# Hardware loops on three engines, and a ring of 96 rows, in an RMSNorm and swish kernel

## The chip, the cores and the metric

The kernel runs on one core of one Trainium2 chip. The metric is the device time of one execution in microseconds (us), of which lower is better. A core has engines that run their own instruction streams and meet at semaphores: TensorE (PE), VectorE (DVE), ScalarE (ACT), GpSimd (POOL) and SyncE (SP), which here only issues transfers. Sixteen DMA engines move data between HBM and the on-chip memories; in this trace every transfer of SP lands in sixteen parts, one for each of them, and the parts land in the order of issue.

## The reference

The input `x` has 16 x 1024 rows of 512 float32 numbers. Each row is normalized by its root mean square, multiplied by `gamma`, and passed through swish:

```python
rms = np.sqrt(np.mean(x ** 2, axis=-1, keepdims=True) + eps)
x_norm = x / rms * gamma
return (x_norm * (1.0 / (1.0 + np.exp(-x_norm)))).astype(np.float32)
```

So 33.55 MB are read and 33.55 MB are written, with little arithmetic on each number.

## The kernel before

**Tiling.** The 16384 rows are laid over 128 partitions, so each partition has 128 rows ("rows" below are these: one row is 128 x 2 KB = 256 KB of data). They come in eight groups of 16 rows per partition, and within a group the 16 rows of a partition lie together in HBM: a transfer of 16 rows has pieces of 32 KB, one of 4 rows has pieces of 8 KB, each 32 KB from the next. `xb` is a ring in SBUF with room for `ring = 100` rows; a row is loaded, worked on in place and stored from its place.

**Transfers.** `loads` and `stores` are lists of (first row, number of rows), and `order` is the order in which SP issues them, all on one queue. `load` (the transfer is issued at L121) makes SP wait for the store that frees the ring's places, and `store` (L127) waits for the swish of the store's last rows. With 100 places, the nine loads of rows 0 to 99 are issued at once, then the three stores of rows 0 to 31, then the three loads of rows 100 to 127, each behind one of these stores, then the other eight stores.

**Units.** `cn = 4` rows are a unit, so there are K = 32 units. For each unit:

- ACT, `square(k)`: waits for the landing, squares two rows with their sums accumulated (L170, output to `junk`, two instructions a row in the profile), and squares the other two rows at once into `sq` in PSUM (L177);
- DVE, `sums(k)`: adds up `sq` (L205) and so completes `ms`;
- POOL: adds `eps` (L151) and raises to the power -0.5 (L158), which gives `rstd`;
- DVE, `norm(k)`: four instructions, one a row, `x * rstd * gamma` (L216);
- ACT, `swish(k)`: Silu over the four rows (L189), in place.

ACT runs `square(k)` and then `swish(k - 2)`; DVE runs `sums(k)` and then `norm(k - 1)`. All of it is written out unit by unit: no engine has a loop at run time, and each wait is for a count that grows with the unit. `ms`, `aeps` and `rstd` have a place for every unit, `sq` and `junk` have two buffers each, and the writers of `sq` and `junk` wait for their former readers (`s_sum`, `s_acc`).

Of the kernel before, what the change touches and what calls it, by code (L numbers as in the profile page):

```python
# [9 lines left out]
def kernel(  # L10
# [7 lines left out]
    nc = tc.nc  # L18
    P = nc.NUM_PARTITIONS
    AF = mybir.ActivationFunctionType  # L20
    ALU = mybir.AluOpType
    fp32 = mybir.dt.float32
# [3 lines left out]
    R, D = xf.shape  # L26

    groups = [16] * 8
    ring = 100
    loads = [(0, 4), (4, 4), (8, 8), (16, 16), (32, 16), (48, 16), (64, 16), (80, 16)]  # L30
    loads += [(96, 4), (100, 12), (112, 12), (124, 4)]
    stores = [(0, 16), (16, 8), (24, 8), (32, 16), (48, 16), (64, 16), (80, 16)]
    stores += [(96, 4), (100, 12), (112, 8), (120, 8)]
    order = [("load", i) for i in range(loads.index((100, 12)))]
    order += [("store", t) for t in range(3)]
    order += [("load", i) for i in range(loads.index((100, 12)), len(loads))]
    order += [("store", t) for t in range(3, len(stores))]
    early = 2
    cn = 4
    n_sq = 2  # L40

    first = [sum(groups[:g]) for g in range(len(groups))]
    rows_each = sum(groups)
# [6 lines left out]
        assert sum(n for _, n in pieces) == rows_each  # L50

    K = rows_each // cn
    landings, seen = [], 0
    for k in range(K):
        landings.append([])
# [6 lines left out]
    inv_d = 1.0 / float(D)  # L62
    eps_f = float(eps)
# [4 lines left out]
    def sbuf(name, shape, dt=fp32):  # L68
        return nc.alloc_sbuf_tensor(name, shape, dt).ap()

    xb = sbuf("xb", [P, ring, D])
    gamma4 = sbuf("gamma4", [P, D])
    gamma_sb = sbuf("gamma_sb", [P, D])
    neg_half = sbuf("neg_half", [P, cn])
    ms = sbuf("ms", [P, K, cn])
    aeps = sbuf("aeps", [P, K, cn])
    rstd = sbuf("rstd", [P, K, cn])
    sq = [nc.alloc_psum_tensor(f"sq{i}", [P, n_sq, D], fp32).ap() for i in range(2)]
    junk = [nc.alloc_psum_tensor(f"junk{i}", [P, D], fp32).ap() for i in range(2)]

    ld = [nc.alloc_semaphore(f"ld{t}") for t in range(len(loads))]
    st = [nc.alloc_semaphore(f"st{t}") for t in range(len(stores))]
    s_gld = nc.alloc_semaphore("s_gld")
    s_zero = nc.alloc_semaphore("s_zero")
    s_half = nc.alloc_semaphore("s_half")
    s_gamma = nc.alloc_semaphore("s_gamma")
    s_acc = nc.alloc_semaphore("s_acc")
    s_sq = nc.alloc_semaphore("s_sq")
    s_sum = nc.alloc_semaphore("s_sum")
    s_eps = nc.alloc_semaphore("s_eps")  # L90
    s_rstd = nc.alloc_semaphore("s_rstd")
    s_norm = nc.alloc_semaphore("s_norm")
    s_swish = nc.alloc_semaphore("s_swish")

    def need(ins, sem, value):
        return ins.wait_op(sem, value, "sem-ge")
# [17 lines left out]
    def load(i):  # L114
        a, n = loads[i]
        for u, (c, m) in enumerate(stores):
            over = c + ring < a + n and a < c + m + ring
            if over and u not in stored_by_sync:
                nc.sync.wait_ge(st[u], 16)
                stored_by_sync.add(u)  # L120
        return nc.sync.dma_start(  # L121
            out=buf(loads[i]), in_=dram(xf, loads[i])
        ).then_inc(ld[i], 16)

    def store(t):
        need(
            nc.sync.dma_start(out=dram(of, stores[t]), in_=buf(stores[t])),  # L127
            s_swish, ends[t],
        ).then_inc(st[t], 16)
# [3 lines left out]
    for t in range(early):  # L133
        ins = load(t).ins
        assert here[-1] is ins or here[-1].name == ins.name
        here.pop()
        at = next(
            i for i, other in enumerate(entry)
            if other.engine == mybir.EngineType.SP
            and isinstance(other, mybir.InstDrain)  # L140
        )
        entry.insert(at, ins)
    for what, t in order[early:]:
        load(t) if what == "load" else store(t)

    nc.gpsimd.memset(gamma4, 0.0).then_inc(s_zero, 1)  # L146
    nc.gpsimd.memset(neg_half, -0.5).then_inc(s_half, 1)  # L147
    nc.gpsimd.wait_ge(s_half, 1)
    for k in range(K):
        need(  # L150
            nc.gpsimd.tensor_scalar(  # L151
                out=aeps[:, k, :], in0=ms[:, k, :], scalar1=eps_f, scalar2=None,
                op0=ALU.add,
            ),
            s_sum, k + 1,
        ).then_inc(s_eps, 1)
        need(
            nc.gpsimd.tensor_tensor(  # L158
                out=rstd[:, k, :], in0=aeps[:, k, :], in1=neg_half, op=ALU.pow
            ),  # L160
            s_eps, k + 1,
        ).then_inc(s_rstd, 1)

    def square(k):
        at = k * cn % ring
        for landing in landings[k]:
            nc.scalar.wait_ge(ld[landing], 16)  # L167
        for j in range(n_sq, cn):
            n = k * (cn - n_sq) + j - n_sq
            acc = nc.scalar.activation(  # L170
                out=junk[n % 2], in_=xb[:, at + j, :], func=AF.Square,
                scale=inv_d**0.5, accum_out=ms[:, k, j : j + 1],
            )
            if n >= 2:
                need(acc, s_acc, n - 1)
            acc.then_inc(s_acc, 1)
        square = nc.scalar.activation(  # L177
            out=sq[k % 2], in_=xb[:, at : at + n_sq, :],
            func=AF.Square, scale=inv_d**0.5,
        )  # L180
        if k >= 2:
            need(square, s_sum, k - 1)
        square.then_inc(s_sq, 1)

    def swish(k):
        at = k * cn % ring
        rows = xb[:, at : at + cn, :]
        need(
            nc.scalar.activation(out=rows, in_=rows, func=AF.Silu), s_norm, k + 1  # L189
        ).then_inc(s_swish, 1)  # L190

    need(
# [1 line left out]
        s_zero, 1,  # L194
    ).then_inc(s_gld, 16)
    nc.scalar.preload_act_table_set("silu_and_others")  # L196
    for k in range(K + 2):
        if k < K:
            square(k)
        if k >= 2:  # L200
            swish(k - 2)

    def sums(k):
        need(
            nc.vector.tensor_reduce(  # L205
                out=ms[:, k, 0:n_sq], in_=sq[k % 2], op=ALU.add,
                axis=mybir.AxisListType.X,
            ),
            s_sq, k + 1,
        ).then_inc(s_sum, 1)  # L210

    def norm(k):
        at = k * cn % ring
        for j in range(cn):
            row = xb[:, at + j, :]
            ins = nc.vector.scalar_tensor_tensor(  # L216
                out=row, in0=row, scalar=rstd[:, k, j : j + 1], in1=gamma_sb,
                op0=ALU.mult, op1=ALU.mult,
            )
            if j == 0:  # L220
                need(ins, s_rstd, k + 1)
        ins.then_inc(s_norm, 1)

    for k in range(K + 1):
        if k < K:
            sums(k)
        if k == 0:
            need(
                nc.vector.stream_shuffle(gamma_sb, gamma4, [0] * 32), s_gld, 16  # L229
            ).then_inc(s_gamma, 1)  # L230
        if k == 1:
            nc.vector.wait_ge(s_gamma, 1)
        if k >= 1:
            norm(k - 1)

    for t in range(len(stores)):
        if t not in stored_by_sync:
# [36 lines left out]
```

## Time and profile before

| what | us |
|---|---|
| median of three runs (lowest, highest) | 161.36 (161.28, 161.55) |
| the profiled execution | 161.94 |
| its span, first to last instruction | 160.6 |
| its last swish ends | 140.42 |
| its last store is issued | 140.4 |

The span is what the profile's views show; 1.3 us of the profiled execution lie outside of it. "DMA share" in a table of windows is the busy time of the transfers' packets over sixteen engines' time; a packet counts where it ends, so a single microsecond may show more than 1. A row such as `q1 hardware_dynamic: 3312, 67.11, 98.1%` gives packets, MB and share of one queue; q1 is SP's. The trace also records when each of a transfer's sixteen parts has landed. For some of the transfers (us from the span's start; first and last part):

| transfer | issued | first part landed | last part landed |
|---|---|---|---|
| load (0, 4) | 0.00 | 4.25 | 4.78 |
| load (32, 16) | 2.76 | 31.14 | 31.55 |
| load (48, 16) | 3.24 | 40.86 | 41.71 |
| load (64, 16) | 3.86 | 50.58 | 51.62 |
| load (80, 16) | 4.38 | 60.28 | 61.34 |
| load (96, 4) | 4.86 | 63.30 | 65.17 |
| store (0, 16) | 30.04 | 72.99 | 74.88 |
| load (112, 12) | 79.75 | 97.31 | 99.20 |
| load (124, 4) | 84.62 | 99.80 | 102.42 |
| store (80, 16) | 109.88 | 138.44 | 141.14 |
| store (112, 8) | 133.82 | 153.03 | 155.73 |
| store (120, 8) | 140.45 | 157.90 | 160.58 |

### The profile page before, as it was taken

To read this page: it belongs to the slowest core of one execution; us is meant where nothing else is said; L and a number is where in the kernel's file an instruction comes from. 1 tells how busy PE (TensorE), PEld (TensorE's weight loads), DVE (VectorE), ACT (ScalarE), POOL (GpSimd) and SP (SyncE) were. 2 spreads that over 40 slices of the span, in tenths; PEclk is the share of its full clock that TensorE was granted. 3 is DMA by queue.
4 is the path that set the end of the run, shared out by engine and by line. 5 is a ranking of instruction groups with operands and counts; after the bars stand their busy time and mean duration, and the time that the engine had idled before them with its cause. 6 is when DMAs were issued, how large, how long until landed. Compare 5 with 4: busy or idle time off the path is not lost.

```text
span 160.6 us, 503 instructions
## 1 busy us (share of the span) xinstructions
DVE 124.5 (78%) x162; ACT 129.6 (81%) x193; POOL 65.4 (41%) x70
## 2 busy tenths in 40 slices
DVE  0287959999999999999999999999999999400000
ACT  1939959999999999999999999999999994700000
POOL 1053545555555555555555555555555555000000
DMA  7999999999999999999999999999999999899993
GB/s 263 449 465 392 498 416 392 481 432 392 453 449 400 424 404 369 459 424 392 426 453 447 410 435 433 435 465 408 424 475 408 400 490 416 369 451 437 428 420 139
DMA packets 3324, 67.15 MB, mean 418 GB/s; under 512 B 372, under 2 KB 372, under 8 KB 376
## 3 DMA queue, kind: packets, MB, share of 16 engines
q1 hardware_dynamic: 3312, 67.11, 98.1%
q14 instruction: 4, 0.03, 0.0%
q10 hardware_dynamic: 8, 0.01, 0.0%
HBM read 33.56 MB, written 33.55 MB: 418 GB/s over the span
## 4 chain that ended last, share of the span: by engine, by line
ACT 63%; DMA 12%; issue 7%; DVE 4%; SPq 0%; ACTq 0%
ACT xb L189 25%; ACT junk L170 22%; ACT sq L177 16%; DMA xb<-in_x_dram 12%; DVE xb L216 3%; DVE ms L205 1%; SPq L121 0%; ACTq L167 0%
## 5 line engine op out<-in xcount | busy, mean ns | idle before, releaser
L216 DVE SCALAR_TENSOR_TENSOR xb<-xb,rstd,gamma_sb 128x512 f32<-128x512 f32 x128 | 87.3, 745 | 0.0
L189 ACT ACTIVATE xb<-xb 128x2048 f32<-128x2048 f32 x32 | 60.9, 1903 | 2.8 <-DVE xb L216 2.8
L205 DVE TENSOR_REDUCE ms<-sq 128x2 f32<-128x1024 f32 x32 | 39.2, 1225 | 14.0 <-ACT sq L177 10.6
L151 POOL TENSOR_SCALAR aeps<-ms 128x4 f32<-128x4 f32 x32 | 20.6, 645 | 65.6 <-DVE ms L205 65.6
L158 POOL TENSOR_TENSOR rstd<-aeps,neg_half 128x4 f32<-128x4 f32 x32 | 44.0, 1376 | 2.7
L170 ACT ACTIVATE junk<-xb 128x512 f32<-128x512 f32 x64 | 37.2, 582 | 4.5 <-DMA xb<-in_x_dram 4.5
L177 ACT ACTIVATE sq<-xb 128x1024 f32<-128x1024 f32 x32 | 32.2, 1005 | 0.0
L170 ACT ACTIVATION_READ_ACCUMULATOR junk<-xb 128x1 f32 x64 | 11.9, 186 | 0.0
L196 ACT ACT_TABLE_LOAD x1 | 1.3, 1283 | 3.6 <-issue 3.6
L146 POOL MEMSET gamma<- 128x512 f32 x1 | 0.5, 525 | 1.5 <-POOLq L66 1.5
L229 DVE STREAM_SHUFFLE gamma_sb<-gamma 128x512 f32<-128x512 f32 x1 | 0.7, 720 | 0.0
L255 POOL MEMSET const-float32-0.0<- 128x1 f32 x1 | 0.1, 99 | 0.2 <-issue 0.2
L255 POOL MEMSET const-bfloat16-1.0<- 128x1 bf16 x1 | 0.1, 102 | 0.0
L255 POOL MEMSET const-uint8-127<- 128x1 uint8 x1 | 0.1, 102 | 0.0
L147 POOL MEMSET neg_half<- 128x4 f32 x1 | 0.1, 102 | 0.0
L255 POOL MEMSET const-float32-1.0<- 128x1 f32 x1 | 0.1, 98 | 0.0
L229 DVE LOAD_MASK_SELECT gamma_sb<-gamma x1 | 0.0, 15 | 0.0
## 6 DMA issues: line engine op xcount, KB each, us to landing
xb<-in_x_dram SPq DMA_DIRECT2D x5, 4096.0 KB, 38.5
out_dram<-xb SPq DMA_DIRECT2D x5, 4096.0 KB, 36.3
out_dram<-xb SPq DMA_DIRECT2D x4, 2048.0 KB, 30.2
xb<-in_x_dram SPq DMA_DIRECT2D x2, 3072.0 KB, 18.2
xb<-in_x_dram SPq DMA_DIRECT2D x4, 1024.0 KB, 12.3
out_dram<-xb SPq DMA_DIRECT2D x1, 3072.0 KB, 25.0
xb<-in_x_dram SPq DMA_DIRECT2D x1, 2048.0 KB, 10.2
out_dram<-xb SPq DMA_DIRECT2D x1, 1024.0 KB, 29.7
```

The lines of the kernel that those rows point to most:

```text
L146: nc.gpsimd.memset(gamma4, 0.0).then_inc(s_zero, 1)
L147: nc.gpsimd.memset(neg_half, -0.5).then_inc(s_half, 1)
L151: nc.gpsimd.tensor_scalar(out=aeps[:, k, :], in0=ms[:, k, :], scalar1=eps_f, scalar2=None, op0=ALU.add,),
L158: nc.gpsimd.tensor_tensor(out=rstd[:, k, :], in0=aeps[:, k, :], in1=neg_half, op=ALU.pow),
L170: acc = nc.scalar.activation(out=junk[n % 2], in_=xb[:, at + j, :], func=AF.Square, scale=inv_d**0.5, accum_out=ms[:, k, j : j + 1],)
L177: square = nc.scalar.activation(out=sq[k % 2], in_=xb[:, at : at + n_sq, :], func=AF.Square, scale=inv_d**0.5,)
L189: nc.scalar.activation(out=rows, in_=rows, func=AF.Silu), s_norm, k + 1
L196: nc.scalar.preload_act_table_set("silu_and_others")
L205: nc.vector.tensor_reduce(out=ms[:, k, 0:n_sq], in_=sq[k % 2], op=ALU.add, axis=mybir.AxisListType.X,),
L216: ins = nc.vector.scalar_tensor_tensor(out=row, in0=row, scalar=rstd[:, k, j : j + 1], in1=gamma_sb, op0=ALU.mult, op1=ALU.mult,)
L229: nc.vector.stream_shuffle(gamma_sb, gamma4, [0] * 32), s_gld, 16
L255: nc = _bacc.Bacc("TRN2", target_bir_lowering=False, num_devices=1)
```

## The change

ACT, DVE and POOL each get a hardware loop (`nc.Fori`) of ten rounds; a round covers `turn = 3` units. The first `lead = 2` squares and the first `sums` stand ahead of the loops, and the last units behind them. Inside a round every semaphore is waited on with a constant from 1 to 3, and at the round's end `take` waits for the full 3 and takes them away again. Since a loop can't name a different landing semaphore in every round, TensorE, which has no other work, waits for each landing in turn and passes it on as a number of units in `s_land`. Addresses in the ring come from registers: `snap` and `bass.ds` make register instructions. In the built program a round has on ACT 11 fused register instructions (each of three to six register operations), 3 single ones, the two takes and a branch beside its 12 activations; on DVE 12 fused and one single one, two takes and a branch; on POOL one register instruction, two takes, a branch, and one instruction that selects the GpSimd library, which stands at the first place in the program that needs it and so falls inside the loop.

The ring must hold a whole number of rounds, so it has 96 rows. The loads (96, 4), (100, 12), (112, 12), (124, 4) become (96, 16), (112, 8), (120, 8), and the stores (96, 4), (100, 12) become (96, 16): ten stores and eleven loads where there were eleven and twelve. `ms`, `aeps`, `rstd` and `sq` have three buffers, and `junk` six, of which four are in SBUF; the waits on `s_sum` and `s_acc` by their writers are gone.

```diff
@@ -26,18 +26,20 @@
     R, D = xf.shape
 
     groups = [16] * 8
-    ring = 100
+    ring = 96
     loads = [(0, 4), (4, 4), (8, 8), (16, 16), (32, 16), (48, 16), (64, 16), (80, 16)]
-    loads += [(96, 4), (100, 12), (112, 12), (124, 4)]
+    loads += [(96, 16), (112, 8), (120, 8)]
     stores = [(0, 16), (16, 8), (24, 8), (32, 16), (48, 16), (64, 16), (80, 16)]
-    stores += [(96, 4), (100, 12), (112, 8), (120, 8)]
-    order = [("load", i) for i in range(loads.index((100, 12)))]
+    stores += [(96, 16), (112, 8), (120, 8)]
+    order = [("load", i) for i in range(loads.index((96, 16)))]
     order += [("store", t) for t in range(3)]
-    order += [("load", i) for i in range(loads.index((100, 12)), len(loads))]
+    order += [("load", i) for i in range(loads.index((96, 16)), len(loads))]
     order += [("store", t) for t in range(3, len(stores))]
     early = 2
     cn = 4
     n_sq = 2
+    turn = 3
+    lead = 2
 
     first = [sum(groups[:g]) for g in range(len(groups))]
     rows_each = sum(groups)
@@ -50,6 +52,9 @@
         assert sum(n for _, n in pieces) == rows_each
 
     K = rows_each // cn
+    assert (K - lead) % turn == 0 and ring % (turn * cn) == 0
+    rounds = (K - lead) // turn
+    per_ring = ring // (turn * cn)
     landings, seen = [], 0
     for k in range(K):
         landings.append([])
@@ -72,11 +77,12 @@
     gamma4 = sbuf("gamma4", [P, D])
     gamma_sb = sbuf("gamma_sb", [P, D])
     neg_half = sbuf("neg_half", [P, cn])
-    ms = sbuf("ms", [P, K, cn])
-    aeps = sbuf("aeps", [P, K, cn])
-    rstd = sbuf("rstd", [P, K, cn])
-    sq = [nc.alloc_psum_tensor(f"sq{i}", [P, n_sq, D], fp32).ap() for i in range(2)]
+    ms = sbuf("ms", [P, turn, cn])
+    aeps = sbuf("aeps", [P, turn, cn])
+    rstd = sbuf("rstd", [P, turn, cn])
+    sq = [nc.alloc_psum_tensor(f"sq{i}", [P, n_sq, D], fp32).ap() for i in range(turn)]
     junk = [nc.alloc_psum_tensor(f"junk{i}", [P, D], fp32).ap() for i in range(2)]
+    junk += [sbuf(f"junk{i}", [P, D]) for i in range(2, turn * (cn - n_sq))]
 
     ld = [nc.alloc_semaphore(f"ld{t}") for t in range(len(loads))]
     st = [nc.alloc_semaphore(f"st{t}") for t in range(len(stores))]
@@ -84,6 +90,7 @@
     s_zero = nc.alloc_semaphore("s_zero")
     s_half = nc.alloc_semaphore("s_half")
     s_gamma = nc.alloc_semaphore("s_gamma")
+    s_land = nc.alloc_semaphore("s_land")
     s_acc = nc.alloc_semaphore("s_acc")
     s_sq = nc.alloc_semaphore("s_sq")
     s_sum = nc.alloc_semaphore("s_sum")
@@ -143,50 +150,53 @@
     for what, t in order[early:]:
         load(t) if what == "load" else store(t)
 
+    def take(queue, sem, n):
+        need(queue.nop(nofuse=True), sem, n).then_inc(sem, -n)
+
+    for i, (a, n) in enumerate(loads):
+        units = (a + n) // cn - max(a // cn, lead)
+        if units > 0:
+            need(nc.tensor.nop(nofuse=True), ld[i], 16).then_inc(s_land, units)
+
     nc.gpsimd.memset(gamma4, 0.0).then_inc(s_zero, 1)
     nc.gpsimd.memset(neg_half, -0.5).then_inc(s_half, 1)
     nc.gpsimd.wait_ge(s_half, 1)
-    for k in range(K):
+
+    def power(k, nth):
+        m = k % turn
         need(
             nc.gpsimd.tensor_scalar(
-                out=aeps[:, k, :], in0=ms[:, k, :], scalar1=eps_f, scalar2=None,
+                out=aeps[:, m, :], in0=ms[:, m, :], scalar1=eps_f, scalar2=None,
                 op0=ALU.add,
             ),
-            s_sum, k + 1,
+            s_sum, nth + 1,
         ).then_inc(s_eps, 1)
         need(
             nc.gpsimd.tensor_tensor(
-                out=rstd[:, k, :], in0=aeps[:, k, :], in1=neg_half, op=ALU.pow
+                out=rstd[:, m, :], in0=aeps[:, m, :], in1=neg_half, op=ALU.pow
             ),
-            s_eps, k + 1,
+            s_eps, nth + 1,
         ).then_inc(s_rstd, 1)
 
-    def square(k):
-        at = k * cn % ring
-        for landing in landings[k]:
-            nc.scalar.wait_ge(ld[landing], 16)
+    def rows(at, n):
+        return xb[:, at : at + n, :] if isinstance(at, int) else xb[:, bass.ds(at, n), :]
+
+    def square(k, at, sem, count, accs):
         for j in range(n_sq, cn):
-            n = k * (cn - n_sq) + j - n_sq
             acc = nc.scalar.activation(
-                out=junk[n % 2], in_=xb[:, at + j, :], func=AF.Square,
-                scale=inv_d**0.5, accum_out=ms[:, k, j : j + 1],
+                out=junk[(k % turn) * (cn - n_sq) + j - n_sq], in_=rows(at + j, 1)[:, 0, :], func=AF.Square,
+                scale=inv_d**0.5, accum_out=ms[:, k % turn, j : j + 1],
             )
-            if n >= 2:
-                need(acc, s_acc, n - 1)
-            acc.then_inc(s_acc, 1)
-        square = nc.scalar.activation(
-            out=sq[k % 2], in_=xb[:, at : at + n_sq, :],
-            func=AF.Square, scale=inv_d**0.5,
-        )
-        if k >= 2:
-            need(square, s_sum, k - 1)
-        square.then_inc(s_sq, 1)
-
-    def swish(k):
-        at = k * cn % ring
-        rows = xb[:, at : at + cn, :]
-        need(
-            nc.scalar.activation(out=rows, in_=rows, func=AF.Silu), s_norm, k + 1
+            if j == n_sq:
+                need(acc, sem, count)
+        nc.scalar.activation(
+            out=sq[k % turn], in_=rows(at, n_sq), func=AF.Square, scale=inv_d**0.5,
+        ).then_inc(s_sq, 1)
+
+    def swish(at, nth):
+        need(
+            nc.scalar.activation(out=rows(at, cn), in_=rows(at, cn), func=AF.Silu),
+            s_norm, nth + 1,
         ).then_inc(s_swish, 1)
 
     need(
@@ -194,44 +204,66 @@
         s_zero, 1,
     ).then_inc(s_gld, 16)
     nc.scalar.preload_act_table_set("silu_and_others")
-    for k in range(K + 2):
-        if k < K:
-            square(k)
-        if k >= 2:
-            swish(k - 2)
-
-    def sums(k):
+    for k in range(lead):
+        assert landings[k] == [k]
+        square(k, k * cn, ld[k], 16, k * (cn - n_sq))
+
+    def sums(k, nth):
         need(
             nc.vector.tensor_reduce(
-                out=ms[:, k, 0:n_sq], in_=sq[k % 2], op=ALU.add,
+                out=ms[:, k % turn, 0:n_sq], in_=sq[k % turn], op=ALU.add,
                 axis=mybir.AxisListType.X,
             ),
-            s_sq, k + 1,
+            s_sq, nth + 1,
         ).then_inc(s_sum, 1)
 
-    def norm(k):
-        at = k * cn % ring
+    def norm(k, at, nth):
         for j in range(cn):
-            row = xb[:, at + j, :]
+            row = rows(at + j, 1)[:, 0, :]
             ins = nc.vector.scalar_tensor_tensor(
-                out=row, in0=row, scalar=rstd[:, k, j : j + 1], in1=gamma_sb,
+                out=row, in0=row, scalar=rstd[:, k % turn, j : j + 1], in1=gamma_sb,
                 op0=ALU.mult, op1=ALU.mult,
             )
             if j == 0:
-                need(ins, s_rstd, k + 1)
+                need(ins, s_rstd, nth + 1)
         ins.then_inc(s_norm, 1)
 
-    for k in range(K + 1):
-        if k < K:
-            sums(k)
-        if k == 0:
-            need(
-                nc.vector.stream_shuffle(gamma_sb, gamma4, [0] * 32), s_gld, 16
-            ).then_inc(s_gamma, 1)
-        if k == 1:
-            nc.vector.wait_ge(s_gamma, 1)
-        if k >= 1:
-            norm(k - 1)
+    sums(0, 0)
+    need(
+        nc.vector.stream_shuffle(gamma_sb, gamma4, [0] * 32), s_gld, 16
+    ).then_inc(s_gamma, 1)
+    nc.vector.wait_ge(s_gamma, 1)
+
+    with nc.Fori(0, rounds, engines=[mybir.EngineType.Activation]) as i:
+        now = nc.scalar.snap((i % per_ring) * (turn * cn))
+        then = nc.scalar.snap(((i + 1) % per_ring) * (turn * cn))
+        for m in range(turn):
+            behind = now + (m + lead) * cn if m + lead < turn else then + (m + lead - turn) * cn
+            square(m + lead, behind, s_land, m + 1, lead * (cn - n_sq) + m * (cn - n_sq))
+            swish(now + m * cn, m)
+        take(nc.scalar, s_land, turn)
+        take(nc.scalar, s_norm, turn)
+    for m in range(lead):
+        swish((rounds * turn + m) * cn % ring, m)
+
+    with nc.Fori(0, rounds, engines=[mybir.EngineType.DVE]) as i:
+        now = nc.vector.snap((i % per_ring) * (turn * cn))
+        for m in range(turn):
+            sums(m + 1, m + 1)
+            norm(m, now + m * cn, m)
+        take(nc.vector, s_sq, turn)
+        take(nc.vector, s_rstd, turn)
+    sums(K - 1, 1)
+    for m in range(lead):
+        norm(rounds * turn + m, (rounds * turn + m) * cn % ring, m)
+
+    with nc.Fori(0, rounds, engines=[mybir.EngineType.Pool]) as i:
+        for m in range(turn):
+            power(m, m)
+        take(nc.gpsimd, s_sum, turn)
+        take(nc.gpsimd, s_eps, turn)
+    for m in range(lead):
+        power(rounds * turn + m, m)
 
     for t in range(len(stores)):
         if t not in stored_by_sync:
```

## The prediction

> **What bounds the kernel now.** I read the chain of waits first, from its end:
>
> ```profile
> 138.49 0.02 issue
> 138.51 1.91 ACT xb L189
> ```
>
> It ends with the last swish, at 140.42, in a span of 160.6. Its shares (ACT 63%) therefore tell what sets the end of the computing, and 20.2 us come after that. The page's DMA rows tell what fills them:
>
> ```profile
> DMA  7999999999999999999999999999999999899993
> q1 hardware_dynamic: 3312, 67.11, 98.1%
> q14 instruction: 4, 0.03, 0.0%
> ```
>
> The DMA engines have work from the first to the last slice. The last store confirms it: issued at 140.45, it landed 20.1 us later, while the load (8, 8), as many rows, landed 4.9 us after the one before it: some 15 us of the 20.1 were queueing. Transfers bound the span, and computing is early. The third view, DMA by windows, shows where the transfers lose time:
>
> ```profile
> core 0: us, DVE busy (x) ACT busy (x) POOL busy (x), PEclk, DMA share, GB/s
> 60.00:64.00 4.00, 3.87 (x6) 4.00 (x7) 2.04 (x2) 1.00 1.06 367
> 64.00:68.00 4.00, 3.87 (x5) 4.00 (x7) 2.05 (x2) 1.00 1.00 430
> ...
> 157.00:158.00 1.00, 0.00 (x0) 0.00 (x0) 0.00 (x0) 1.00 0.73 311
> 158.00:159.00 1.00, 0.00 (x0) 0.00 (x0) 0.00 (x0) 1.00 0.08 33
> 159.00:160.00 1.00, 0.00 (x0) 0.00 (x0) 0.00 (x0) 1.00 0.08 33
> ```
>
> From 158 on a share of 0.08 is 1.3 of 16 engines: nearly all are done, and one or two late ones set the end. And from 60 to 64 the engines are fully busy but move 367 GB/s, where the next window moves 430: packets take longer for their bytes. That is the load (96, 4).
>
> **What one late engine costs.** The table of landings ahead gives the last part of each transfer. Sixteen rows take 9.72 us from one to the next (stores too, 65.17 to 74.88: 9.71), so 0.607 us a row. Against this:
>
> - (96, 4): 61.34 to 65.17, 3.83 for four rows where 2.43 is the pace. Excess 1.40. The first parts are late too (60.28 to 63.30, 3.02, excess 0.59), so all engines lose there. In the trace's packets, its 8 KB packets take up to 1029 ns where most others take 309.
> - (124, 4): 99.20 to 102.42, 3.22. Excess 0.79, nearly all on the latest engine: one packet of 1020 ns (0.71 over 309).
> - (48, 16) and (64, 16): 31.55 to 41.71 and to 51.62, 10.16 and 9.91. Excess 0.44 and 0.19. Two of the four q14 packets, 8192 bytes of instructions each, stand here, at 40.4 and 44.1, and packets behind them took 1576 and 1875 ns where 1213 is usual. The others, at 77.2 and 119.8, delayed engines that were not the latest.
>
> Together 2.82 us on the latest engine.
>
> **The change, part by part.**
>
> *Lists of transfers.* No load or store of four rows is left but the two at the start. The rows 96 to 99 now come as part of 32 KB pieces, which ran at 1213 to 1228 ns wherever nothing stood in the way, and 124 to 127 in 16 KB pieces, which took 611. That takes away 1.40 and 0.79, if the short pieces are the cause. Two transfers fewer save two 9 ns semaphore packets an engine and some 6 ns for each 8 KB packet (309 less a quarter of 1213): below 0.15, taken as 0.
>
> *Instruction fetch.* Between ACT's first fetch (40.4) and the one at 119.8 ACT has 125 recorded instructions; the first comes behind 64, DVE's only one (44.1) behind 50, POOL's (77.2) behind 53. In the changed program ACT's loop ends at about its 55th instruction, DVE's at its 43rd, POOL's at its 33rd. So no engine should come to a fetch before its loop is over, late in the run, and a round on ACT (35 instructions) is small beside the 125. That takes away 0.44 + 0.19.
>
> [...]
>
> *Ring of 96 and the order on SP.* Rows 96 to 99 used to be loaded ahead of the first stores; now they come behind stores of 32 rows. After load (80, 16) at 61.34 the queue holds those stores (19.4 us), which frees load (96, 16) when the first of them lands near 71; it lands near 90.5. ACT squares these rows at 101.8, so 11 us are left. The loads (112, 8) and (120, 8), freed near 76 and 81, are needed at 117.7 and 125.7 and land near 95 and 100. Each of the three is issued while at least 4.9 us of other rows are queued, and the stores behind them on SP (from row 32) were ready since about 78 or are needed after 100. The queue never runs empty. Cost 0.
>
> *Loops.* The trace shows no register instruction. The nearest rows on the same sequencers are semaphore instructions, 17 ns (21 on DVE); the farthest is SP's issue of a load, 425 ns. They run ahead of the engine's work: ACT's wait at 36.096 was passed 6 ns after the swish of 36.09 began, and that swish ran 1.91. ACT's round has 17 such instructions: at most two between a swish and the square behind it, and six where the branch lies between (takes, counter, branch, a fused and a single register instruction). At 17 ns each all is hidden. At 425 the six take 2.55 us and exceed the swish's 1.9 us cover by 0.65, or 5.9 us over nine rounds. On DVE 425 ns stand beside each 0.66 us norm, and the four at the round's end beside 2.73 us of norms: hidden. I take the low end, since a register operation is nearer to a semaphore instruction than to building a transfer. The takes wait for counts that the round's last unit has waited for already, so they hold up only themselves; behind them stand the next square (ACT), the next sum (DVE), the next `eps` (POOL). TensorE's waits delay nothing but the landings that they pass on, in order.
>
> What is the cover worth? The very first load, unqueued, had its 4 rows landed at 4.78; with four more, 7.2. The last store, issued at 140.45, could come 160.6 - 7.2 - 140.45 = 13 us later before it alone set today's end, 11 us for the end that I forecast. A unit takes ACT 3.99 us, so the computing may lengthen by 0.4 us a unit, 1.2 a round. All that happens to `junk`, `sq` and their waits lies under this too.
>
> *GpSimd's library.* It was selected once, at 2.41 (two records of 11 ns); now ten times. The first `eps` at 8.45 started 0.09 us after the sum it needs, so the selection took between 0.02 and 6.0 us. What a round can hide is read from the timeline:
>
> ```profile
> 117.31 0.66 POOL L151 TENSOR_SCALAR aeps<-ms 128x4 f32<-128x4 f32 x1 [1.85 <-DVE ms L205]
> 118.05 1.39 POOL L158 TENSOR_TENSOR rstd<-aeps,neg_half 128x4 f32<-128x4 f32 x1
> 121.14 2.73 DVE L216 SCALAR_TENSOR_TENSOR xb<-xb,rstd,gamma_sb 128x512 f32<-128x512 f32 x4
> ```
>
> POOL idles 1.85 before a unit, and its result, ready at 119.44, is used at 121.14: 1.85 + 1.70 = 3.55 us. I take the low end: no packet of another queue than SP's and the one for gamma was moved between 2.4 and 8.45, so nothing was loaded from HBM by the DMA engines.
>
> [...]
>
> **The sum.** Span: 61.34 - 0.63 + 160 rows x 0.607 = 157.8, which is 2.8 below today. No engine can end sooner than the first one does now, 157.90 less its 0.59 at (96, 4): 157.3, so the sum is not beyond what is there. But a packet that took 0.7 too long (1875, 1029, 1020 ns) came three times in this run, and the new 16 KB loads stand at the same changeover from loads to stores. I leave one in: 0.8. So 2.0 us, against the profiled 161.94: 159.9, and against the median of 161.36: 159.4.
>
> **Rivals.**
>
> 1. *The late packets belong to the changeover, not to the four-row pieces.* For it: both stand where loads end and stores begin. Against: the 32 KB packets on either side keep their 1213, and at the second changeover the first parts kept pace (97.31 to 99.80, 2.49). Then only the fetches go: 161.36 - 0.6 = 160.8, or nothing: 161.4.
> 2. *GpSimd reselects its library in earnest each round (slower).* Place: the first `eps` of each round. Price: at the 6.0 us bound, 6.0 - 3.55 = 2.45 us on some 8.5 rounds, 20.8; the last store is issued at 161.3 and lands at 168.5, which is 169.2. It decides only if a selection costs over 3.55 + 13 / 8.5 = 5.1 us; below that computing is later and the end is not. The register instructions would need 1.5 us a round exposed to do the same. For it: ten selections are in the program. Against: no transfer for it in the trace.
> 3. *The loops don't keep their instructions, and each backward branch fetches.* Thirty packets of 0.31 us; if one DMA engine has them all, 9.3 us on the forecast: 168.7. Against: the counts above.
>
> **How the numbers follow.** Forecast (158.4 to 160.3, by zero to three late packets) 0.58; below that 0.04; rival 1 0.20, of which 0.09 is faster, 0.09 the same and 0.02 slower; rival 2 0.10, and rival 3 with any other loss in the loops 0.08, of which 0.01 the same. A measurement of this kernel tells about 0.2% (0.3 us) from no change. Faster 0.71, same 0.10, slower 0.19. The range 158.4 to 161.8 takes in the forecast and rival 1 and leaves out the slow rivals and the lowest case.
>
> **What would show it.** Right: the load (96, 16) and the store after it land 9.7 us apart; one q14 packet or none before 130; the last parts within 1 us of each other; the last swish still near 140, ACT's unit near 3.99. Wrong: windows with full share and under 400 GB/s at the changeovers (rival 1), POOL idle before L168 in every third unit by more than 1.9 us with the last swish past 150 (rival 2), q14 in the tens (rival 3).

## The result, and the profile after

| | before | after |
|---|---|---|
| median of five runs (lowest, highest), us | 161.55 (161.28, 161.70) | 160.90 (160.63, 160.98) |
| ratio of the times, 95% interval | | 0.9959 (0.9945 to 0.9974) |
| second session, medians, us | 161.69 | 160.58 |
| its ratio, 95% interval | | 0.9932 (0.9916 to 0.9949) |
| profiled execution, us | 161.94 | 160.9 |
| its span; last part of the last store landed, us | 160.6; 160.58 | 159.4; 159.33 |

The change makes the kernel 0.4 to 0.7% faster, 0.65 to 1.1 us. I had forecast 2.0. The direction is right and the time lies in the range; the size is a third to just over a half of what I gave. The profiled execution of before stood 0.6 above the median of its own runs (161.36), that of after on its median, so the two traces differ by more (1.25 us in the last landing) than the medians do.

The page of after, its span, DMA row and queues:

```profile
span 159.4 us, 900 instructions
DMA  7999999999999999999999999999999999999896
q1 hardware_dynamic: 3024, 67.11, 98.8%
q14 instruction: 1, 0.00, 0.0%
```

The transfers still bound the span. The one q14 packet has 32 bytes and stands at 0.01 us: no instructions were fetched in the run. The recorded instructions rose from 503 to 900, a number that will matter. The end of the chain of waits is where it was:

```profile
138.53 0.02 issue
138.55 1.91 ACT xb L198
```

The last swish ends at 140.46 (140.42 before), so the computing did not lengthen. DMA by windows, at the first changeover and at the end:

```profile
core 0: us, DVE busy (x) ACT busy (x) POOL busy (x), PEclk, DMA share, GB/s
57.00:61.00 4.00, 3.90 (x6) 4.00 (x7) 2.04 (x2) 1.00 1.06 344
61.00:65.00 4.00, 3.86 (x6) 4.00 (x7) 2.05 (x2) 1.00 1.02 442
...
157.00:158.00 1.00, 0.00 (x0) 0.00 (x0) 0.00 (x0) 1.00 0.62 262
158.00:159.00 1.00, 0.00 (x0) 0.00 (x0) 0.00 (x0) 1.00 0.04 16
159.00:160.00 1.00, 0.00 (x0) 0.00 (x0) 0.00 (x0) 1.00 0.00 0
```

Two things are to be seen. The slow stretch ahead of the first store is still there: full share and 344 GB/s, now in a load of 16 rows with pieces of 32 KB. And from 158 on one engine is late (0.04 is 0.6 of sixteen) where there were two. The landings tell the rest:

| transfer | last part landed | after the one before | over the pace | first part landed |
|---|---|---|---|---|
| load (48, 16) | 41.28 | 9.71 | 0 | 40.78 |
| load (64, 16) | 50.99 | 9.71 | 0 | 50.49 |
| load (80, 16) | 61.62 | 10.62 | 0.91 | 61.00 |
| store (0, 16) | 71.29 | 9.68 | 0 | 70.70 |
| load (96, 16) | 90.76 | | | 90.11 |
| load (112, 8) | 95.66 | 4.91 | 0.05 | 95.01 |
| load (120, 8) | 100.56 | 4.89 | 0.03 | 99.90 |
| store (32, 16) | 110.44 | 9.88 | 0.17 | 109.57 |
| store (80, 16) | 139.92 | | | 138.56 |
| store (120, 8) | 159.33 | | | 157.95 |

The fetches' 0.63 in (48, 16) and (64, 16) is gone and the second changeover costs next to nothing, but (80, 16) has an excess of 0.91. A new loss is spread over the stores from (32, 16) to (80, 16): 9.88, 9.84, 9.86 and 9.77 us each on the latest engine, where the first parts keep 9.67. It stops when the computing stops at 140.

### The profile page after: what moved, and what is told of

Same layout as the page of the kernel before. It is cut to its first block, busy times and chain, and to the rows that moved or that the text cites. A ratio compares the mean times of both kernels' runs of the same rounds, so it can differ in the third digit from the quotient of the medians.

```text
span 159.4 us, 900 instructions
## 1 busy us (share of the span) xinstructions
DVE 124.5 (78%) x162; ACT 129.6 (81%) x193; POOL 65.4 (41%) x70
## 3 DMA queue, kind: packets, MB, share of 16 engines
q1 hardware_dynamic: 3024, 67.11, 98.8%
## 5 line engine op out<-in xcount | busy, mean ns | idle before, releaser
L223 DVE SCALAR_TENSOR_TENSOR xb<-xb,rstd,gamma_sb 128x512 f32 (+1 forms) x128 | 87.3, 744 | 0.0
L198 ACT ACTIVATE xb<-xb (+1 forms) x32 | 60.9, 1902 | 2.8 <-DVE xb L223 2.8
L168 POOL TENSOR_SCALAR aeps<-ms 128x4 f32<-128x4 f32 x32 | 20.6, 644 | 65.6 <-DVE ms L213 65.6
L175 POOL TENSOR_TENSOR rstd<-aeps,neg_half 128x4 f32<-128x4 f32 x32 | 44.1, 1377 | 2.7
L186 ACT ACTIVATE junk<-xb 128x512 f32 (+1 forms) x64 | 38.6, 603 | 4.5 <-PEq L159 4.4
L192 ACT ACTIVATE sq<-xb 128x1024 f32 (+1 forms) x32 | 32.1, 1005 | 0.0
```

Of the source, the lines that this page charges most:

```text
L168: nc.gpsimd.tensor_scalar(out=aeps[:, m, :], in0=ms[:, m, :], scalar1=eps_f, scalar2=None, op0=ALU.add,),
L175: nc.gpsimd.tensor_tensor(out=rstd[:, m, :], in0=aeps[:, m, :], in1=neg_half, op=ALU.pow),
L186: acc = nc.scalar.activation(out=junk[(k % turn) * (cn - n_sq) + j - n_sq], in_=rows(at + j, 1)[:, 0, :], func=AF.Square, scale=inv_d**0.5 ...
L192: nc.scalar.activation(out=sq[k % turn], in_=rows(at, n_sq), func=AF.Square, scale=inv_d**0.5,).then_inc(s_sq, 1)
L198: nc.scalar.activation(out=rows(at, cn), in_=rows(at, cn), func=AF.Silu),
L223: ins = nc.vector.scalar_tensor_tensor(out=row, in0=row, scalar=rstd[:, k % turn, j : j + 1], in1=gamma_sb, op0=ALU.mult, op1=ALU.mult,)
```

## The experiments

The table has every run that was timed; the ratio is to the kernel before in the same session. "(80, 16)" is that load's time behind the one before it; this column and the last landing are from the profiled execution alone. In four of the kernels another transfer meets the first store; their sections give its time.

| run | median us | ratio, 95% interval | (80, 16) | last landing |
|---|---|---|---|---|
| lists_only | 161.62 | 0.9998 (0.9982 to 1.0014) | 11.22 | 160.00 |
| four_rows | 160.71 | 0.9940 (0.9917 to 0.9963) | | 159.05 |
| store_early | 161.17 | 0.9958 (0.9941 to 0.9975) | 9.72 | 159.61 |
| touch_out | 160.59 | 0.9936 (0.9913 to 0.9958) | 10.54 | 159.20 |
| after_again | 160.58 | 0.9932 (0.9916 to 0.9949) | 10.70 | 159.25 |
| fetch_loads | 163.27 | 1.0102 (1.0085 to 1.0119) | 11.41 | 161.62 |
| fetch_stores | 162.45 | 1.0051 (1.0034 to 1.0068) | 10.42 | 160.90 |
| touch_sp | 160.84 | 0.9953 (0.9936 to 0.9970) | 10.51 | 159.28 |
| store_four | 161.10 | 0.9961 (0.9943 to 0.9979) | 9.71 | 159.63 |
| store_act_timed | 160.64 | 0.9919 (0.9897 to 0.9940) | 9.72 | 159.23 |
| more_instr | 161.62 | 0.9989 (0.9971 to 1.0007) | 10.60 | 160.11 |

### lists_only: the lists without the loops

The kernel before, with after's ring, loads and stores:

```diff
-    ring = 100
+    ring = 96
-    loads += [(96, 4), (100, 12), (112, 12), (124, 4)]
+    loads += [(96, 16), (112, 8), (120, 8)]
-    stores += [(96, 4), (100, 12), (112, 8), (120, 8)]
+    stores += [(96, 16), (112, 8), (120, 8)]
     ...                  # order: loads.index((96, 16)) for loads.index((100, 12))
```

> The kernel before, written out without loops, with the changed kernel's ring of 96 rows and its lists of loads and stores; nothing else is changed. It parts the lists from the loops. If the gain lies in the lists (the four-row loads gone), it runs at 0.996 of before and within 0.2 us of the changed kernel. If it lies in the instruction fetches that the loops do away with, it runs at 0.999 to 1.000, its trace shows four instruction packets of 8192 bytes in the run, and the last part of the load in flight at each fetch lands 0.4 us or more late. Both can hold: then it lies between, near 0.998. The loss of 0.8 us ahead of the first store is there in either case.

The lists alone bring nothing: the interval lies about 1. The four instruction packets are back (40.6, 44.3, 77.7, 120.0), (48, 16) takes 10.39 and (80, 16), without a four-row piece near it, 11.22. The 16-row stores behind it keep 9.65 to 9.71. Its queue row and the window of the first store:

```profile
q14 instruction: 4, 0.03, 0.0%
57.00:61.00 4.00, 3.90 (x6) 4.00 (x7) 2.04 (x2) 1.00 1.06 360
```

So the measured gain is the loops', and most of my forecast (2.19 of 2.82) stood on the wrong part of the change.

### four_rows: the loops with the four-row loads

```diff
-    ... (64, 16), (80, 16)]
+    ... (64, 16), (80, 12), (92, 4)]
-    loads += [(96, 16), (112, 8), (120, 8)]
+    loads += [(96, 16), (112, 12), (124, 4)]
```

> The changed kernel with four-row loads put back at both changeovers from loads to stores: (80, 16) is split into (80, 12) and (92, 4), and (112, 8), (120, 8) become (112, 12), (124, 4). If four-row pieces are themselves slow, the latest part of (92, 4) lands 3.8 us behind that of (80, 12), 1.4 over its pace, that of (124, 4) 3.2 us behind (112, 12), 0.8 over, and the run is about 1.2 us slower than the changed kernel (1.003 of before). If the loss belongs to the changeover whatever the pieces are, the loss ahead of the first store is 0.9 as in the changed kernel, none stands at (124, 4), and the time is that of the changed kernel within 0.3 us.

The other half of the same test. In windows, the two changeovers:

```profile
57.00:61.00 4.00, 3.90 (x6) 4.00 (x7) 2.04 (x2) 1.00 1.00 344
97.00:101.00 4.00, 3.90 (x6) 4.00 (x7) 2.05 (x2) 1.00 1.10 465
```

The load (92, 4) took 3.21 us, an excess of 0.78, which is no more than the 0.91 of after's 16-row load: the same 344 GB/s with pieces of 8 KB or of 32. (124, 4) took 2.47, an excess of 0.04. The time is that of after. At these two places four-row pieces cost nothing that can be told from 16-row ones.

### store_early and store_four: the first store moved

The first store is cut in two and its first part issued ahead of the loads (64, 16) and (80, 16); in the second kernel it has four rows and stands ahead of (48, 16).

```diff
-    stores = [(0, 16), (16, 8), ...
+    stores = [(0, 8), (8, 8), (16, 8), ...
     ...
-    order = [("load", i) for i in range(loads.index((96, 16)))]
-    order += [("store", t) for t in range(3)]
+    order = [("load", i) for i in range(loads.index((64, 16)))]
+    order += [("store", 0)]
+    order += [("load", i) for i in range(loads.index((64, 16)), loads.index((96, 16)))]
+    order += [("store", t) for t in range(1, 4)]
     ...
```

> The changed kernel with its first store cut into (0, 8) and (8, 8), and (0, 8) issued ahead of the loads (64, 16) and (80, 16), so that the queue changes from loads to stores twice before row 96: near 41 us and near 66 us. If the loss is paid once, ahead of the first store of the run, the latest part of (48, 16) lands about 0.9 us over the pace of 9.71 and (80, 16) keeps its pace; the time is that of the changed kernel. If each change from loads to stores costs it, both are late and the time is 0.8 us longer. If the loss hangs on the place in the run or in the input (rows 92 to 95), it stays at (80, 16).

> The changed kernel with its first store cut into (0, 4) and (4, 12), and the four rows issued among the loads, ahead of (48, 16), so that the first store of full pieces is a short one (8 KB pieces) near 31 us. If the loss of 0.8 to 0.9 us is a fixed price of the first store, it stands at the load (32, 16), which lands 0.9 over its pace, and the time is that of the changed kernel (0.993 to 0.996). If it grows with the size of the first store, less than half of it shows there and the rest is gone: 0.5 us faster, 0.990 to 0.992. If it needs a store of 32 KB pieces, it stays at (80, 16).

Windows of store_early:

```profile
38.00:42.00 4.00, 3.86 (x6) 4.00 (x7) 2.04 (x3) 1.00 0.95 295
57.00:61.00 4.00, 3.90 (x6) 4.00 (x7) 2.04 (x2) 1.00 0.99 426
```

The slow stretch went with the store, to 38 to 42 us, and left 57 to 61 at 426 GB/s. It is paid once in the run: (48, 16), now just ahead of the first store, took 10.59 (excess 0.88), and (80, 16) the bare 9.72. In store_four it moved to (32, 16) (10.83, excess 1.1), for a store of four rows. So it is the price of the first store of the run, whatever is loaded ahead of it, and a smaller first store does not make it smaller.

### touch_out and touch_sp: a tiny write ahead of it

Sixteen bytes a partition are written to the output early, over ACT's queue or over SP's; the first store waits for them, and overwrites them.

```diff
     ...                                       # touch_sp; ahead of load (32, 16):
+            need(
+                nc.sync.dma_start(out=dram(of, (0, 1))[:, 0, 0:cn], in_=neg_half),
+                s_half, 1,
+            ).then_inc(s_touch, 16)
+        if (what, t) == ("store", 0):
+            nc.sync.wait_ge(s_touch, 16)
```

> The changed kernel with one more transfer on ScalarE's queue at the start: 16 bytes in each of 128 partitions, from a constant, into the first row of each of the first 128 pieces of the output; the first store waits until it has landed and overwrites it. All sixteen DMA engines so write to the output long before the first store. If the loss ahead of the first store is the price of the first write to the output, it moves to the start, where it delays only this transfer, the load (80, 16) keeps its 9.71 us, and the run is 0.8 us faster than the changed kernel (0.991 of before). If it comes from loads and stores meeting in the queue, (80, 16) stays 0.9 over and the time is that of the changed kernel.

> The changed kernel with the 16-byte writes to the output on SP's own queue, behind the load (16, 16), instead of on ScalarE's. The loss ahead of the first store stayed where it was when another queue had written to the output before. If it belongs to the first store of this queue, whatever its size, it now stands near 21 us, and (80, 16) keeps its pace of 9.71; the time is that of the changed kernel. If it belongs to the first store of full size, (80, 16) stays 0.9 over.

Both landed before 23 us, and (80, 16) took 10.54 and 10.51 all the same. So neither a first write to the output nor a first write on the queue is what costs, as far as writes of 16 bytes can show it.

### after_again: the changed kernel once more

> The changed kernel once more, unaltered, as the measure for the three beside it: 0.996 of before, no instruction packet in the run, the latest part of (80, 16) about 0.9 over its pace.

The same landings: 10.70 at (80, 16), no instruction packet, the latest engine 0.62 behind the next at the end (159.25 and 158.63).

### fetch_loads and fetch_stores: fetches put back

128 semaphore instructions in SP's stream, between stores that are issued from 30 to 49 us, or from 94 to 120 us. They bring two fetches each. No transfer is moved; the 256 added instructions are the one other difference.

```diff
+        if (what, t) in [('store', 0), ('store', 1)]:      # fetch_stores: 5 and 6
+            for _ in range(128):
+                need(nc.sync.nop(nofuse=True), ld[0], 16).then_inc(s_acc, 1)
```

> The changed kernel with 128 semaphore instructions that wait for nothing put into SP's stream behind its first store (30 us) and again behind its second (38 us), where SP has nothing to do; no transfer is moved. They make SP's instruction stream long enough for two fetches during the loads, ahead of the changeover. If the fetches are what the loops save, the trace shows two packets of 8192 bytes between 30 and 50 us, the latest engine is 0.4 to 1.0 us behind the others at (64, 16) and 1.4 to 2.2 at the first store, and the run is 0.6 us or more slower than the changed kernel, at 0.999 to 1.000 of before. If something else in the loops makes the gain, it runs like the changed kernel, 0.996.

> As the one with the instructions among the loads, but behind the stores (64, 16) and (80, 16), at 94 and 110 us, so that the two fetches fall among the stores, behind the changeovers. If a fetch costs only its own time on one DMA engine, the latest engine loses 0.3 to 0.6 us and the run is 0.997 to 0.999 of before; if the cost is made at the first changeover, where an engine that is already late falls back further, it is less than with the fetches among the loads, and the run stays near 0.996.

fetch_loads is 2.7 us above after_again. The queue row and the end of its span:

```profile
q14 instruction: 2, 0.02, 0.0%
```

```profile
158.00:159.00 1.00, 0.00 (x0) 0.00 (x0) 0.00 (x0) 1.00 0.08 33
159.00:160.00 1.00, 0.00 (x0) 0.00 (x0) 0.00 (x0) 1.00 0.08 33
160.00:161.00 1.00, 0.00 (x0) 0.00 (x0) 0.00 (x0) 1.00 0.04 16
```

One late engine makes the end: 161.62, where the next has done at 158.46. In the packets it can be followed. Each fetch (39.4 and 48.6) took 0.31 us on it, and the 32 KB packet behind took 1628 ns and not 1213: 0.73 us a fetch, 1.06 behind the next engine at (64, 16). Then it met the first store, and one packet there took 3042 ns where the others took near 2000: 2.11 behind at (80, 16). In fetch_stores the two fetches (102.5 and 118.3), past the first store, cost 0.64 each, and the last landing is 1.65 above after_again's. The other 0.4 fits the added instructions: around the fetches the packets of one engine took 1274 to 1321 ns while they ran. In fetch_loads they cost nothing of that kind: from 30 to 57 us no 32 KB packet but the two behind the fetches took over 1230 ns. So a fetch here cost its 0.64 to 0.73 us on its engine, and the lateness it made grew by as much again, from 1.06 to 2.11, where the first store was still ahead.

### store_act: the first store on another queue

lists_only, with its first store cut into (0, 8) and (8, 8), and (0, 8) issued by ACT at 22.4 us; store_act is a single execution (160.76), store_act_timed the same kernel timed.

```diff
     ...
+        if k == 4:
+            store(0, nc.scalar)
```

> The kernel before without loops, with the new lists, its first store cut into (0, 8) and (8, 8), and (0, 8) issued by ScalarE on its own queue as soon as its swish is done (about 24 us), so that it runs between the loads instead of behind them. If the loss is a price of the first store of full pieces, on whatever queue, the loads in flight near 24 to 32 us land late by more than the store's own 4.9 us, and (80, 16) keeps its pace of 9.71. If it comes only from SP's own queue changing from loads to stores, (80, 16) is late by 0.8 to 0.9 as before.

> The kernel without loops, with the new lists and its first store, (0, 8), on ScalarE's queue at 22 us, once more and timed. It makes the four instruction fetches of the kernel before, but the price of the first store is paid before them, while all engines are level. If a fetch costs only its own 0.7 us on one engine, this runs like the kernel without loops and with the new lists, 0.9998 of before. If most of its cost is made at the first store, where an engine that is already late falls back further, it runs near the changed kernel, 0.993 to 0.997.

The loss moved with the store, over to another queue: the first parts of the 40 rows behind load (16, 16) took 25.04 us for 24.28, and (80, 16) again 9.72. The window where the other kernels are slow is not slow here:

```profile
57.00:61.00 4.00, 3.90 (x6) 4.00 (x7) 2.04 (x2) 1.00 1.16 500
```

The time surprised me. This kernel has no loops and its four fetches (40.2 to 120.8), and is as fast as after: 0.9919 and 0.9932 can't be told apart. In it the price of the first store is paid before the fetches have made an engine late. That fits fetch_loads: much of what a fetch costs in the kernel before is paid at the first store. It is an argument from two kernels that differ in more than this, not a separate test.

### more_instr: more instructions, no other work

```diff
+    for _ in range(256):
+        need(nc.tensor.nop(nofuse=True), ld[0], 16).then_inc(s_acc, 1)
```

They stand in TensorE's stream behind the last landing, and ran from 100 to 140 us.

> The changed kernel with 256 semaphore instructions that wait for nothing behind TensorE's last landing, from about 100 us; TensorE has nothing else to do. In the changed kernel one DMA engine alone falls back by 0.2 us in each of the 16-row stores from (32, 16) to (64, 16), 0.6 in all, which the kernels without loops show by about half and which ends when the computing ends. If this goes with the number of instructions that are executed and recorded, the latest engine falls back by 1 us or more between 100 and 130 us and the run is at least 0.4 us slower than the changed kernel. If not, its landings are as in the changed kernel and the time is too. A fetch for TensorE's own stream would show as an instruction packet of 8192 bytes and is counted apart, at 0.7 us.

The end in windows:

```profile
157.00:158.00 1.00, 0.00 (x0) 0.00 (x0) 0.00 (x0) 1.00 0.65 279
158.00:159.00 1.00, 0.00 (x0) 0.00 (x0) 0.00 (x0) 1.00 0.12 49
159.00:160.00 1.00, 0.00 (x0) 0.00 (x0) 0.00 (x0) 1.00 0.04 16
```

Two engines are late now. One had a fetch (16384 bytes on q8 at 133.7, while TensorE ran the added instructions; 986 ns, and 1613 ns for the packet behind it) and lost 1.37 us to it, but is not the latest. The latest is the one that drifts: its stores from (32, 16) on took 10.01, 10.10, 10.08 and 9.99, and it ends at 160.11 against 159.25. So 256 instructions cost 0.86 us, some 3.4 ns each, on one DMA engine; the ratio rose from 0.9932 to 0.9989, which is 0.9 us. Whether the instructions themselves do that or what is recorded of them stays open.

### before_again: a second profile of the kernel before

> The kernel before, unaltered, with a second profile. If the excess of 0.79 us at the load (124, 4) belongs to the kernel, its latest part again lands 3.2 us behind that of (112, 12). If it was an accident of the first profile, it lands 2.4 to 2.5 behind it, and the span is shorter by some 0.5 us or more. The excesses at (48, 16) and (64, 16), with two instruction packets near 40 and 44 us, and 1.4 on the latest engine at (96, 4), should come again in either case.

A single execution (161.64). (96, 4) took 3.67, an excess of 1.24; its latest engine was 0.47 behind the next ahead of it and 0.97 behind it. (124, 4) took 2.73, an excess of 0.30 where the first profile had 0.79. The last part landed at 160.29, not 160.58.

## Why the prediction was right in direction and wrong in size

The two kernels' latest engines, term by term, from the two profiles the result rests on:

| term | forecast gain | gain in the traces |
|---|---|---|
| excess at (96, 4) | 1.40 | 1.40 - 0.91 = 0.49 |
| excess at (124, 4) | 0.79 | about 0.74, of which 0.49 is not in before_again |
| instruction fetch | 0.63 | 0.63 |
| a late packet left in | -0.8 | in the first term |
| drift of one engine | not in the sum | -0.61 |
| sum | 2.0 | 1.25 (last landings: 160.58 - 159.33) |

The 0.8 that I left in for a late packet happened to cover nearly all of the 0.91 that stayed at the first store, and that is luck: I had not meant it for a price that comes in every run. So the 0.77 between 2.02 and 1.25 is the drift (0.61) and small terms (0.16); against the medians (0.65 to 1.1) the 0.49 that the second profile of the kernel before does not have comes on top.

**What bounds the kernel, and the end that counts.** Right: the transfers bound both kernels (98.1% and 98.8% of sixteen engines' time), and one late engine sets the end. That is why half a microsecond on one engine of sixteen is measurable.

**Excess at (96, 4), the step that failed.** I put 1.40 down to the four-row pieces, "if the short pieces are the cause". They are not (four_rows, lists_only): 0.91 still stands at the same place in the changed kernel, without a short piece. That is the price of the first store, which every kernel here paid once on all engines: 0.7 to 1.1 us on the latest engine where the engines were level, 0.5 to 1.0 on the first part to land. Rival 1 is nearly true for this term (it is the first store and not every changeover), and the sign that I had named for it was there: full share and 367 GB/s before, 344 after. My objection, that the 32 KB packets on either side kept 1213 ns, held because (96, 4) was the last load ahead of the store and so took the whole loss. The other 0.49 went, but for another reason: by fetch_loads and lists_only it was the further falling back of an engine that fetches had made late.

**Excess at (124, 4), mis-sized.** One packet of 1020 ns in one profile, taken for a property of the transfer. A second profile has 0.30. What made the packet late stays open.

**Instruction fetch.** Right in mechanism and size: 0.63 went, and there were no fetches before 130, nor any later. The fetch packets carry a time, a size and a queue, and not the engine they were for: which were ACT's, DVE's and POOL's was my estimate from the counts. What I missed is that this term does not add to the first but drives part of it. The end of the computing did not move with the fetches: the last swish ended at 140.42 with four of them and at 140.46 with none. But in this program, bound by DMA, a fetch of 8192 bytes took 0.4 to 1.0 us from a data engine (0.98 for the one at 44.1, whose next packet took 1875 ns, 0.42 for the one at 119.8).

**The drift, the term that was missing.** I counted register instructions only as time on their own sequencers. On the latest engine the stores (32, 16) to (80, 16) keep 9.65 to 9.71 in lists_only with its 500 instructions, take up to 9.88 with 900, and up to 10.10 with 1156. Behind the last load, 58.16 us to the end (102.42 to 160.58) became 58.77 (100.56 to 159.33), so 0.61 was taken back. The packets show that the drift was there before, too. Between 103 and 138 us, packets that took 6 to 80 ns more than the usual 1213 add up to 0.27 us in before and 0.28 in lists_only, with 112 and 110 recorded instructions in that stretch, to 0.52 in after with 204, and to 1.35 in more_instr with 432: 2.4 to 3.1 ns for each. In the kernel before they fell on engines that were not the latest and cost nothing at the end; in the changed kernel, without fetches, the other engines are level (last parts from 157.95 to 158.55) and the drifting one is the latest.

**Lists, ring and SP's order at 0.** Right. The queue did not run empty (a 9 in slices 2 to 37 of the DMA row of after), and (96, 16) landed at 90.76 where I had 90.5.

**Register instructions at the low end.** Right that they are hidden; their size lies between my bounds. On ACT they took 35 to 136 ns each (fused ones 52 to 136, a compare and branch 40 to 50), on DVE 36 to 125. ACT's round-end instructions ran from 107.99 to 108.93, inside the swish of 107.98 to 109.89. With the takes that is 17 to 136 ns where I had bounds of 17 and 425; a round's 0.94 us leaves 0.96 of the cover.

**GpSimd's library at the low end.** Right. Rival 2 would need POOL idle for more than 1.9 us ahead of a round's first `eps`. POOL in the timeline over two such units:

```profile
97.41 0.66 POOL L168 TENSOR_SCALAR aeps<-ms 128x4 f32<-128x4 f32 x1 [1.89 <-DVE ms L213]
98.15 1.39 POOL L175 TENSOR_TENSOR rstd<-aeps,neg_half 128x4 f32<-128x4 f32 x1
...
101.38 0.66 POOL L168 TENSOR_SCALAR aeps<-ms 128x4 f32<-128x4 f32 x1 [1.84 <-DVE ms L213]
...
105.39 0.66 POOL L168 TENSOR_SCALAR aeps<-ms 128x4 f32<-128x4 f32 x1 [1.89 <-DVE ms L213]
```

The idle time is 1.84 to 1.89 in 28 of the 32 units (65.6 us over all of them, as before the change), the bracket names DVE's sum as what ended it, and the selections stand in the trace as records of 5 to 11 ns. The 6.0 us that the forecast's bound left open for a selection appear in none of the nine rounds behind the first: selecting the same library again added no idle time, and what it may take is hidden in gaps of less than 1.9 us.

**Rival 3.** Did not come: no fetch in thirty rounds.

**The chances.** 0.71 for faster came true by the fetch and not by the main term. Rival 1, which I gave 0.20, priced the fetches alone at 160.8, and that is 0.1 from the measured 160.90: taken as the likeliest it would have been the better forecast, but that is luck in part: two terms that I did not see (0.5 more at the first store, 0.6 less by the drift) nearly cancel.

## What to carry to other kernels

In a kernel bound by DMA, follow the latest of the sixteen engines: compare the first and the last part of each landing, and credit a change only with what it takes from that engine. A transfer that is slow at a changeover need not be slow by its shape (0.78 us over the pace in four_rows with pieces of 8 KB, 0.91 in after with 32); move it, or look whether the whole stretch has full share and low GB/s, before its excess goes into a sum. Instructions are traffic too: here a fetch took 0.4 to 1.0 us from a data engine, and an engine that met the first store 1.06 us late came out 2.11 late (fetch_loads).

## What the runs showed of the hardware

- The first store of a run cost the loads ahead of it time on all sixteen engines, 0.7 to 1.1 us on the latest where the engines were level: in the changed kernel the slow 32 KB packets from 57 to 61 us took 1358 to 2178 ns for 1213. It was paid once, on SP's queue or ACT's, with four rows, eight or sixteen, and 16-byte writes did not prepay it ((80, 16) took 10.54 and 10.51 us behind them). Why is open.
- An engine that was already late lost up to 1.05 us more there (fetch_loads).
- A fetch of 8192 bytes cost one DMA engine 0.4 to 1.0 us (0.64 to 0.73 in fetch_loads and fetch_stores): 0.31 to 0.33 for itself, the rest in the packet behind. One of 16384 bytes, in more_instr, cost 1.37.
- Loops whose round has 35 instructions on ACT, and fewer on the others, ran ten rounds in after without one fetch.
- An added semaphore instruction cost one DMA engine about 3.4 ns while stores ran (more_instr), and 256 of them among the loads slowed no packet (fetch_loads). Why only then, and through what, was not settled.
